# RG-LRU gate products as four 64x64 quadrants of one weight operand, with the halves exchanged on ScalarE

## The chip, the core and the metric

One core of a Trainium2 chip runs the whole program. Its engines are TensorE (PE in the profile; its weight loads are PEld), VectorE (DVE), ScalarE (ACT), GpSimd (POOL) and SyncE (SP). The metric is the device time of one execution in microseconds (us), as the median of three runs.

## The reference

A trunk of two layers over 512 latent and 256 context tokens (768 together), model width 1024. Each layer runs three bidirectional token mixers (HGRN2, mLSTM, RG-LRU), merges them, and then a SwiGLU network. The RG-LRU is 512 channels wide; its gates are block-diagonal products with 8 blocks of 64 channels, for 2 directions (z in the einsum, `d` in the kernel) and 2 gates (g in the einsum, `z` in the kernel: 0 is r, 1 is i):

```
xc = depthwise_conv(lru_x, conv_w, conv_b)
gates = einsum('btnd,zgnde->zgbtne', xc.reshape(b, t, 8, 64), lru_gate_w)   # 2 x 2 gates
gates = gates + lru_gate_b
log_a = -8 * softplus(-lam) * sigmoid(r_pre);  a = exp(log_a)
u = sqrt(max(-expm1(2 * log_a), 0)) * (sigmoid(i_pre) * xc)
h_t = a_t * h_{t-1} + u_t          # forward and backward
```

All data are float32.

## The kernel before

The kernel keeps channels on the 128 partitions and tokens along the free dimension; a line of 768 tokens is cut into 512 and 256 (`ALL`), each in one PSUM bank. Large projections (`dense`, product at L390, tiles `acc`; and `proj_tok`, product at L500) split each float32 operand into two reduced-precision parts and issue three products per tile of weights (`wh` with the high part, `wh` with the low part, `wl` with the high part).

A layer's mixers come one after the other in the program text: four HGRN2 heads (parts `hg`), four RG-LRU blocks of 128 channels (`lru(0)` to `lru(3)`, parts `lru0` to `lru3`; each holds two of the 64-channel blocks), then the gate projections and state preparation of the mLSTM (part `mg`) and the mLSTM (part `ml`). They don't run strictly one after the other: a list scheduler orders the instructions of each engine ahead of time by their readiness and priority, so that projections of the next block lie between the small products of the one before.

In `lru(i)`: the projection to `x` (eviction at L792), a convolution on VectorE into `xc` (tile tag `F`), then the gates. The weight tile `wg` (tag `th`, 128 x 4 x 128) is cleared by GpSimd (L801) and filled on its diagonal by two DMAs, one for each 64-channel block: for each of the four pairs (d, z) a 128x128 matrix with two 64x64 blocks on its diagonal. The product at L812 multiplies it by `xc` in float32 without a split, once per (d, z) and piece of tokens, into a bank of tag `pl` (two buffers, `pl_...` in the rows); ScalarE evicts it with a sigmoid and its bias (L813) into `sg[d][z]` (tag `K`). So a block `i` issues 4 products of 512 columns and 4 of 256, 64 products in all over two layers. After the gates come exp (L819), tanh (L820), square root (L828) on ScalarE, multiplications and scans on VectorE. ScalarE loads another function table (ACT_TABLE_LOAD) whenever the next function isn't in the one that it holds.

The gate biases come in with other per-channel vectors: `vec_dma` (L172) puts 64 rows of 128 into a staging tile, one DMA per vector, and a transpose makes columns of it. Layer 0's DMAs are issued by GpSimd at the start, those of layer 1 some 60 us later; the first gate that needs them starts at 315 us (layer 0) and 1771 us (layer 1).

Other names in the rows: L733 and L750 and L767 are HGRN2 products (tag `mx`), L742 its eviction; L839 evicts the projection of the output gate, L843 its tanh; L881 to L927 prepare the mLSTM's states (L889 and L927 transpose on TensorE, L904 is VectorE's work ahead of L927); L977 and L1002 are the mLSTM's products with 64-channel operands; L1054 is the merge and the SwiGLU network; L210 and L212 split weights.

Of the kernel before, what the change touches and what calls it, by code (L numbers as in the profile page):

```python
# [12 lines left out]
AF = mybir.ActivationFunctionType  # L13
# [33 lines left out]
def trunk_kernel(ctx: ExitStack, tc: tile.TileContext, a: dict, out: bass.AP):  # L47
# [13 lines left out]
    def nm(p):  # L61
        n_names[0] += 1
        return f"{part[0]}{p}{n_names[0]}"
# [3 lines left out]
    def S(tag, n=T, dt=F32, p=128):  # L67
        return pool[0].tile([p, n], dt, tag=tag, name=nm(tag), bufs=BUFS[tag])
# [11 lines left out]
    def small(n, tag, p=128, dt=F32, bufs=4):  # L80
        return sm.tile([p, n], dt, tag=tag, name=nm(tag), bufs=bufs)
# [4 lines left out]
    def mx(dt=F32):  # L86
        return pp.tile([128, 512], dt, tag="mx", name=nm("mx"), bufs=2)

    def pl(dt=F32):
        return pp.tile([128, 512], dt, tag="pl", name=nm("pl"), bufs=2)  # L90
# [11 lines left out]
    V, ACT, G, PE = nc.vector, nc.scalar, nc.gpsimd, nc.tensor  # L102
# [4 lines left out]
    def ldg(o, i):  # L107
        nc.gpsimd.dma_start(o, i)
# [39 lines left out]
    vec = [{}, {}]  # L148
    negb, halfb = [None, None], [None, None]
    vtiles = []  # L150
    for l in range(2):
# [11 lines left out]
        for i, sp_ in enumerate(specs):  # L163
            n = sum(s[2] for s in sp_)
            vt_ = const.tile([128, n], F32, name=f"vec{l}{i}")
            vtiles.append((sp_, vt_, n))
            r = 0
# [4 lines left out]
    def vec_dma(i, q=ld):  # L172
        sp_, vt_, n = vtiles[i]
        st = small(128, "vst", bufs=2)
        r = 0
        for name, src, k in sp_:
            q(st[r:r + k], src)
            r += k
        return st

    def vec_load(i, st=None):
        _, vt_, n = vtiles[i]
        st = st or vec_dma(i, ldg)
        ps = pl()
        PE.transpose(ps[:, :n], st[:n], ident[:n, :n])
        V.tensor_copy(vt_, ps[:, :n])

    ps = pl()
# [12 lines left out]
    V.tensor_reduce(sel, ident.rearrange("p (g m) -> p m g", g=4)[:, 0:2, :], axis=AX.X, op=OP.add)  # L201
    aw_load(0)
    vst0 = vec_dma(0)
    aw_load(2)
    tok_load(0, 2)
# [190 lines left out]
    ALL = ((0, 512), (512, 256))  # L396
# [123 lines left out]
    v0_load(1)  # L520
    vbs = [load_vb(0)]
    vsts = {i: vec_dma(i, ldg) for i in (2, 1)}
    norm_scale(0, 0, 0, 4)
    st_transpose(0, 0)
# [42 lines left out]
    def layer(l, hh, hl):  # L567
# [217 lines left out]
        gw = a["lru_gate_w"][l]  # L785

        def lru(i):
# [5 lines left out]
            xc = S("F")  # L793
            cw = lambda j: vec[l]["conv_w"][:, j * 4 + i:j * 4 + i + 1]
            V.tensor_scalar(xc, x, cw(2), vec[l]["conv_b"][:, i:i + 1], op0=OP.mult, op1=OP.add)
            for s0, s1 in ((0, CTX), (CTX, T)):
                for j, dlt in ((0, -2), (1, -1), (3, 1)):
                    o0, o1 = s0 + max(0, -dlt), s1 - max(0, dlt)
                    V.scalar_tensor_tensor(xc[:, o0:o1], x[:, o0 + dlt:o1 + dlt], cw(j), xc[:, o0:o1], op0=OP.mult, op1=OP.add)
            wg = S("th", 512).rearrange("p (z c) -> p z c", z=4)  # L800
            G.memset(wg, 0.0)  # L801
            for b in range(2):
                ldg(wg[64 * b:64 * b + 64, :, 64 * b:64 * b + 64],
                   gw[:, :, 2 * i + b].rearrange("d z n e -> n (d z) e"))
            sg = []
            for d in range(2):
                sg.append((S("K"), S("K")))
                for z in range(2):
                    bi = (d * 2 + z) * 4 + i
                    for off, n in ALL:  # L810
                        ps = pl()
                        PE.matmul(ps[:, :n], wg[:, 2 * d + z], xc[:, off:off + n], start=True, stop=True)  # L812
                        ACT.activation(sg[d][z][:, off:off + n], ps[:, :n], AF.Sigmoid, bias=vec[l]["gate_b"][:, bi:bi + 1])  # L813
            hs = []
            for d in range(2):
                s_r, s_i = sg[d]
# [19 lines left out]
            th = t2  # L836
# [12 lines left out]
        for i in range(4):  # L849
            lru(i)  # L850
# [34 lines left out]
        for Gx, R in ((Gi, Ri), (Gf, Rf)):  # L885
            for g in range(2):
                ps = mx()
# [35 lines left out]
        for nm_, R in (("cC", Ri), ("cW", Rf), ("cE", m_)):  # L923
            ct = S("col", NCH * 64)
            ps = mx()
# [107 lines left out]
        def B(tag, dt=F32):  # L1033
            return S(tag, no, dt)
# [50 lines left out]
        for n_, (br, zs) in enumerate(((0, za), (2, zc), (1, zb))):  # L1085
            part[0] = f"L{l}br{br}_"
            bh, bl = [], []
            for i in range(4):
                z = B("zt")
# [36 lines left out]
        for m in range(NK):  # L1126
            x = B("bh")
            if l == 0:
# [3 lines left out]
                for g in range(2):  # L1132
                    ps = pl()
# [20 lines left out]
        for off, n in (GA, GB):  # L1154
            st = Stat(n, no)
# [84 lines left out]
        for off, n in (GA, GB):  # L1240
            if l == 0:
                st = Stat(n, no)
# [24 lines left out]
            else:  # L1267
# [5 lines left out]
                for c in range(2):  # L1273
                    cb_ = (off - 256) // GR + 16 * c
                    for hf in range(2):
                        o = og[c][hf]
# [40 lines left out]
```

## Time and profile before

| | |
|---|---|
| median of 3 runs | 2607.26 us (2605.45 to 2610.02) |
| the profiled execution | 2610.73 us |
| its span in the trace | 2609.0 us |
| TensorE busy | 2532.6 us, 97% of the span |
| VectorE / ScalarE / GpSimd busy | 1561.8 / 961.0 / 110.8 us |
| first and last gate product, layer 0 | 315.7 and 400.3 us |
| first and last gate product, layer 1 | 1771.0 and 1859.6 us |

The busy share of an engine is an average over stages with different limits; the stage of the gates is read from its own stretch. Each float32 product is two records ("x2") in the trace. Records of matmuls overlap, since they are pipelined: how long a group really occupies TensorE is read from the start of one row to the start of the next, not from the duration in the row. An idle time stands behind a row in brackets with what ended it.

### The profile page before, as it was taken

What the parts mean: (1) busy time and instruction counts of PE and PEld (TensorE: products, weight loads), DVE (VectorE), ACT (ScalarE), POOL (GpSimd) and SP (SyncE); (2) the same over time, 40 slices, a digit from 0 to 9 for tenths busy, and PEclk for the clock granted to TensorE, in tenths of its full rate; (3) what the DMA queues carried; (4) which work ended last, traced back from release to release, by engine and by line L of the source; (5) the groups of instructions that cost most, each with busy time, mean ns of one, the idle gap of its engine ahead of it and who ended that gap; (6) DMA issues with size and microseconds to landing.
All of it is one profiled execution on the core that took longest, in us unless ns stands there. A gap on an engine that the chain in (4) does not pass through costs nothing.

```text
span 2609.0 us, 36171 instructions
## 1 busy us (share of the span) xinstructions
PE 2532.6 (97%) x14491; PEld 2193.7 (84%) x14491; DVE 1561.8 (60%) x2959; ACT 961.0 (37%) x1462; POOL 110.8 (4%) x213
## 2 busy tenths in 40 slices
PE   8999999998999999999999989999999999999998
PEld 5999878777888888888888889987877889888887
DVE  4677797463666467557445465787865356633335
ACT  4435484232222343212212254448733234422223
POOL 1000010110000100000000010001011000000000
PEclk9999999999999999999999999999999999999999
DMA  7333233433455343335335254653455455333323
GB/s 244 58 47 53 49 66 62 81 77 102 141 130 117 115 128 117 102 105 162 113 107 157 83 127 65 60 57 61 65 86 122 111 107 175 109 97 97 97 91 112
DMA packets 247480, 264.42 MB, mean 101 GB/s; under 512 B 12328, under 2 KB 213360, under 8 KB 247312
## 3 DMA queue, kind: packets, MB, share of 16 engines
q1 hardware_dynamic: 236464, 227.75, 37.8%
q0 software_dynamic: 10272, 33.31, 4.1%
q8 instruction: 114, 1.87, 0.3%
q10 hardware_dynamic: 576, 1.05, 0.1%
q14 instruction: 54, 0.44, 0.1%
HBM read 249.91 MB, written 12.16 MB: 100 GB/s over the span
## 4 chain that ended last, share of the span: by engine, by line
PE 54%; issue 4%; DVE 3%; ACT 2%; DMA 1%; POOL 0%; POOLq 0%; ACTq 0%; DVEq 0%
PE L0ffn_acc L1054 20%; PE L1ffn_acc L1054 14%; PE L1br_acc L1054 5%; PE L1hg_acc L390 4%; PE L0out_acc L1054 2%; PE L1mg_acc L500 1%; PE L1hg_pl L711 1%; PE L1ml_acc L390 1%; PE L1lru_acc L390 1%; PE L1out_acc L1054 1%; PE L1v_acc L500 1%; PE L1lru_pl L812 0%; PE L1ml_mx L1014 0%; ACT L0ffn_ny L376 0%; DMA L0ffn_d<-L1lru_o 0%
## 5 line engine op out<-in xcount | busy, mean ns | idle before, releaser
L1054 PE MATMUL L0ffn_acc<-L0out_h,L0ffn_wh 128*128 128x512 f32 (+1 forms) x1408 | 348.0, 339 | 0.5 <-DVE L0out_h L381 0.3
L1054 PEld LDWEIGHTS L0ffn_acc<-L0out_h,L0ffn_wh 128*128 128x128 f32 x1408 | 241.9, 190 | 30.5 <-DVE L0out_h L381 0.7
L1054 PE MATMUL L0ffn_acc<-L0out_h,L0ffn_wl 128*128 128x512 f32 (+1 forms) x704 | 236.5, 337 | 0.0
L1054 PE MATMUL L1ffn_acc<-L1out_h,L1ffn_wh 128*128 128x512 f32 (+1 forms) x736 | 219.8, 381 | 1.8 <-ACT L1out_h L380 0.9
L258 DVE SCALAR_TENSOR_TENSOR ada_ny<-ada_w,csk,ada_ny 128x512 f32<-128x512 f32 x224 | 157.4, 747 | 85.5 <-DMA ada_w<-in_w_ada_dram 84.7
L1054 PE MATMUL L0br_acc<-h,L0br_wh 128*128 128x512 f32 (+1 forms) x768 | 191.5, 340 | 0.0
L210 ACT ACTIVATE L0ffn_wh<-L0ffn_w 128x1024 fp32r<-128x1024 f32 (+1 forms) x76 | 77.1, 1014 | 275.0 <-PE L0ffn_acc L1054 224.7
L212 DVE TENSOR_TENSOR L1ffn_wl<-L1ffn_w,L1ffn_wh 128x1024 fp32r<-128x1024 f32 (+1 forms) x76 | 88.8, 1168 | 141.8 <-ACT L1ffn_wh L210 141.0
L1054 PE MATMUL L0ffn_acc<-L0ffn_hid,L0ffn_wh 128*128 128x256 f32 (+1 forms) x704 | 172.7, 338 | 0.0
L1054 PEld LDWEIGHTS L1ffn_acc<-L1out_h,L1ffn_wh 128*128 128x128 f32 x736 | 136.3, 188 | 28.8 <-DVE L1out_h L381 1.3
L210 ACT ACTIVATE L1ffn_wh<-L1ffn_w 128x1024 fp32r<-128x1024 f32 (+1 forms) x76 | 77.2, 1015 | 197.4 <-PE L1ffn_acc L1054 156.9
L1054 PEld LDWEIGHTS L0br_acc<-h,L0br_wh 128*128 128x128 f32 x768 | 132.1, 190 | 16.8 <-issue 0.3
L1054 PEld LDWEIGHTS L0ffn_acc<-L0out_h,L0ffn_wl 128*128 128x128 f32 x704 | 133.3, 190 | 14.2
L1054 PE MATMUL L1ffn_acc<-L1out_h,L1ffn_wl 128*128 128x512 f32 (+1 forms) x368 | 139.6, 380 | 0.0
L212 DVE TENSOR_TENSOR L0ffn_wl<-L0ffn_w,L0ffn_wh 128x1024 fp32r<-128x1024 f32 (+1 forms) x68 | 80.9, 1190 | 94.1 <-ACT L0ffn_wh L210 93.7
L390 PE MATMUL L0hg_acc<-h,L0hg_wh 128*128 128x384 f32 (+2 forms) x512 | 136.1, 343 | 0.0
L1054 PEld LDWEIGHTS L0ffn_acc<-L0ffn_hid,L0ffn_wh 128*128 128x128 f32 x704 | 121.0, 190 | 14.2
L1054 PE MATMUL L0br_acc<-h,L0br_wl 128*128 128x256 f32 (+1 forms) x384 | 129.7, 338 | 0.0
L1054 PE MATMUL L1br_acc<-L0ffn_h,L1br_wh 128*128 128x512 f32 x384 | 121.2, 394 | 1.5 <-ACT L1br_gt L1073 1.5
L1054 PE MATMUL L1ffn_acc<-L1ffn_hid,L1ffn_wh 128*128 128x512 f32 (+1 forms) x448 | 115.4, 347 | 0.0
L390 PE MATMUL L1hg_acc<-L0ffn_h,L1hg_wh 128*128 128x384 f32 (+1 forms) x384 | 107.9, 360 | 0.0
L1054 PE MATMUL L0ffn_acc<-L0ffn_hid,L0ffn_wl 128*128 128x256 f32 (+1 forms) x304 | 102.4, 337 | 0.0
(710 smaller groups left out, 5910.1 us busy)
## 6 DMA issues: line engine op xcount, KB each, us to landing
ada_w<-in_w_ada_dram SPq DMA_DIRECT2D x80, 512.0 KB, 3.7
L0ffn_w<-in_w_ffn_in_dram SPq DMA_DIRECT2D x44, 512.0 KB, 3.6
L1ffn_w<-in_w_ffn_in_dram SPq DMA_DIRECT2D x44, 512.0 KB, 3.5
L0br_w<-in_w_in_dram SPq DMA_DIRECT2D x24, 512.0 KB, 5.6
L1br_w<-in_w_in_dram SPq DMA_DIRECT2D x24, 512.0 KB, 5.4
L0hg_w<-in_w_in_dram SPq DMA_DIRECT2D x16, 512.0 KB, 8.4
L0out_w<-in_w_out_dram SPq DMA_DIRECT2D x16, 512.0 KB, 3.5
L0ffn_w<-in_w_ffn_out_dram SPq DMA_DIRECT2D x16, 512.0 KB, 3.4
```

The lines of the kernel that those rows point to most:

```text
L210: ACT.activation(wh[:, :n], w[:, :n], AF.Copy)
L212: V.tensor_tensor(wl[:, :n], w[:, :n], wh[:, :n].bitcast(F32), op=OP.subtract)
L258: V.scalar_tensor_tensor(ac[i], wv, csk[:, kk, i:i + 1], ac[i], op0=OP.mult, op1=OP.add)
L390: PE.matmul(ps[:, :n], A[:, k, :], B[k][:, off - ao:off - ao + n], start=(i == 0), stop=(i == 3 * nk - 1))
L500: PE.matmul(ps[:, :n], A[k][:, c * 128:(c + 1) * 128], W[:, k % 4, :], start=k == 0 and i == 0, stop=k == 7 and i == 3 * (k1 - k0) - 1)
L711: PE.matmul(pv[:, j * 128:(j + 1) * 128], ks[:, j * 128:(j + 1) * 128], comp(Q[g], c, j, j + 1), start=True, stop=True)
L1054: PE.matmul(ps[:, :n], A[:, k, sl], Bm[k0 + k][:, off - ao:off - ao + n], start=cnt[key] == 0, stop=cnt[key] == tot - 1)
```

## The change

The gate weights of a block now stay 64 wide: `wg` is 128 x 4 x 64, the first 64 partitions holding one 64-channel block and the other 64 the second. There is nothing to clear, so the memset is gone. Each 128x128 product becomes two 64x64 quadrants, which use 64 partitions of the operand and 64 columns of the array. For the r gate (z = 0) block b writes its own half of the bank (the quadrants on the diagonal); for the i gate (z = 1) block b writes the other half (the quadrants beside the diagonal), so that the four quadrants of one (d, piece of tokens) are four different parts of the array. The r gate is evicted by one sigmoid over 128 partitions as before; the i gate by two sigmoids over 64 partitions each, which put the halves back in place. The bias of the i gate lies with exchanged halves too, so `vec_dma` loads it in pieces: six DMAs in place of one in each layer. The loops are nested the other way: pieces of tokens outside, gates inside.

```diff
         for name, src, k in sp_:
-            q(st[r:r + k], src)
+            if name == "gate_b":
+                for d in range(2):
+                    o = r + 8 * d
+                    q(st[o:o + 4], src[8 * d:8 * d + 4])
+                    for h in range(2):
+                        q(st[o + 4:o + 8, 64 * h:64 * h + 64], src[8 * d + 4:8 * d + 8, 64 - 64 * h:128 - 64 * h])
+            else:
+                q(st[r:r + k], src)
...
-            wg = S("th", 512).rearrange("p (z c) -> p z c", z=4)
-            G.memset(wg, 0.0)
+            wg = S("th", 256).rearrange("p (z c) -> p z c", z=4)
             for b in range(2):
-                ldg(wg[64 * b:64 * b + 64, :, 64 * b:64 * b + 64],
-                   gw[:, :, 2 * i + b].rearrange("d z n e -> n (d z) e"))
+                ldg(wg[64 * b:64 * b + 64], gw[:, :, 2 * i + b].rearrange("d z n e -> n (d z) e"))
             sg = []
             for d in range(2):
                 sg.append((S("K"), S("K")))
-                for z in range(2):
-                    bi = (d * 2 + z) * 4 + i
-                    for off, n in ALL:
-                        ps = pl()
-                        PE.matmul(ps[:, :n], wg[:, 2 * d + z], xc[:, off:off + n], start=True, stop=True)
-                        ACT.activation(sg[d][z][:, off:off + n], ps[:, :n], AF.Sigmoid, bias=vec[l]["gate_b"][:, bi:bi + 1])
+                for off, n in ALL:
+                    pz = [pl() for z in range(2)]
+                    for z in range(2):
+                        for b in range(2):
+                            o = 64 * (b ^ z)
+                            PE.matmul(pz[z][o:o + 64, :n], wg[64 * b:64 * b + 64, 2 * d + z], xc[64 * b:64 * b + 64, off:off + n],
+                                      start=True, stop=True)
+                    gb = lambda z: vec[l]["gate_b"][:, (d * 2 + z) * 4 + i:(d * 2 + z) * 4 + i + 1]
+                    ACT.activation(sg[d][0][:, off:off + n], pz[0][:, :n], AF.Sigmoid, bias=gb(0))
+                    for b in range(2):
+                        o = 64 * (1 - b)
+                        ACT.activation(sg[d][1][64 * b:64 * b + 64, off:off + n], pz[1][o:o + 64, :n], AF.Sigmoid, bias=gb(1)[o:o + 64])
```

In the changed kernel every line below L172 stands 7 lower up to the gates (L390 is L397, L500 is L507); the gate product is L818, the sigmoid of the r gate L821, that of the i gate L824. The new code is ordered by the same scheduler, and each engine's order changes around the gates.

TensorE, layer 0, second block, before (`F` is `xc`, `th` the weights, `acc` the projection of the next blocks): the first six gate products.

```order
L390 MATMUL L0lru_acc_3557<-h_149,L0lru_wh_3552 128x512
L812 MATMUL L0lru_pl_3314<-L0lru_F_3300,L0lru_th_3308 128x512
L812 MATMUL L0lru_pl_3317<-L0lru_F_3300,L0lru_th_3308 128x256
L390 MATMUL L0lru_acc_3557<-h_157,L0lru_wh_3552 128x512
L390 MATMUL L0lru_acc_3557<-h_149,L0lru_wl_3553 128x512
L812 MATMUL L0lru_pl_3320<-L0lru_F_3300,L0lru_th_3308 128x512
L812 MATMUL L0lru_pl_3323<-L0lru_F_3300,L0lru_th_3308 128x256
```

The same place after, where "64x512 x2" is two quadrants in one bank:

```order
L397 MATMUL L0lru_acc_3494<-h_149,L0lru_wl_3464 128x256
L818 MATMUL L0lru_pl_3334<-L0lru_F_3321,L0lru_th_3329 64x512 x2
L818 MATMUL L0lru_pl_3335<-L0lru_F_3321,L0lru_th_3329 64x512 x2
L397 MATMUL L0lru_acc_3494<-h_150,L0lru_wh_3463 128x256
L397 MATMUL L0lru_acc_3494<-h_158,L0lru_wh_3463 128x256
L397 MATMUL L0lru_acc_3494<-h_150,L0lru_wl_3464 128x256
L397 MATMUL L0lru_acc_3494<-h_151,L0lru_wh_3463 128x256
L818 MATMUL L0lru_pl_3343<-L0lru_F_3321,L0lru_th_3329 64x256 x2
L397 MATMUL L0lru_acc_3494<-h_159,L0lru_wh_3463 128x256
```

The four quadrants of 512 columns stand together here, those of 256 in two places with 128-wide products between them.

ScalarE at the same gates, layer 0, second block, before (`K` holds the evicted gates):

```order
L813 ACT_TABLE_LOAD
L813 ACTIVATE L0lru_K_3312<-L0lru_pl_3314,vec_89 128x512
L813 ACTIVATE L0lru_K_3312<-L0lru_pl_3317,vec_89 128x256
L843 ACTIVATE L0lru_sd_3362<-L0lru_sd_3362 128x768
L813 ACTIVATE L0lru_K_3313<-L0lru_pl_3320,vec_89 128x512
L813 ACTIVATE L0lru_K_3313<-L0lru_pl_3323,vec_89 128x256
L819 ACT_TABLE_LOAD
```

and after (L830 is the exponential, L819 before; L799 the eviction of the projection, L217 a split of weights):

```order
L821 ACT_TABLE_LOAD
L821 ACTIVATE L0lru_K_3332<-L0lru_pl_3334,vec_89 128x512
L824 ACTIVATE L0lru_K_3333<-L0lru_pl_3335,vec_89 64x512 x2
L821 ACTIVATE L0lru_K_3332<-L0lru_pl_3343,vec_89 128x256
L830 ACT_TABLE_LOAD
L830 ACTIVATE L0lru_Q_3372<-L0lru_K_3332,nsp_1835 128x768
L824 ACT_TABLE_LOAD
L824 ACTIVATE L0lru_K_3333<-L0lru_pl_3344,vec_89 64x256
L799 ACTIVATE L0lru_q_3461<-L0lru_acc_3494,vec_90 128x256
L217 ACTIVATE L0lru_wh_3794<-L0lru_w_3793 128x1024
L824 ACTIVATE L0lru_K_3333<-L0lru_pl_3344,vec_89 64x256
```

The exponential of the r gate, with its table, now stands between the two pieces of the i gate, and the last half follows two other instructions.

TensorE, layer 1, the last gate products before (`mg_acc` is the projection for the mLSTM):

```order
L812 MATMUL L1lru_pl_16243<-L1lru_F_16209,L1lru_th_16217 128x512
L500 MATMUL L1mg_acc_16505<-L1mg_wh_16492,L0ffn_h_12922 128x272
L500 MATMUL L1mg_acc_16505<-L1mg_wl_16493,L0ffn_h_12914 128x272
L500 MATMUL L1mg_acc_16505<-L1mg_wh_16492,L0ffn_h_12915 128x272
L500 MATMUL L1mg_acc_16505<-L1mg_wh_16492,L0ffn_h_12923 128x272
L812 MATMUL L1lru_pl_16246<-L1lru_F_16209,L1lru_th_16217 128x256
```

and the last two places after:

```order
L818 MATMUL L1lru_pl_16338<-L1lru_F_16296,L1lru_th_16304 64x256 x2
L397 MATMUL L1ml_acc_16883<-L0ffn_h_12972,L1ml_wl_16879 128x512
L397 MATMUL L1ml_acc_16883<-L0ffn_h_12973,L1ml_wh_16878 128x512
L397 MATMUL L1ml_acc_16883<-L0ffn_h_12981,L1ml_wh_16878 128x512
L818 MATMUL L1lru_pl_16339<-L1lru_F_16296,L1lru_th_16304 64x256 x2
```

Before, 139 projection products of `mg_acc` followed the last gate; after, the last gates stand behind all of them, in the first projection of the mLSTM.

## Rows read from the trace of the kernel before

**Rows 1.** The page: busy time and share of an engine; the chain of work that ended last.

```profile
PE 2532.6 (97%) x14491; PEld 2193.7 (84%) x14491; DVE 1561.8 (60%) x2959; ACT 961.0 (37%) x1462; POOL 110.8 (4%) x213
...
PE 54%; issue 4%; DVE 3%; ACT 2%; DMA 1%; POOL 0%; POOLq 0%; ACTq 0%; DVEq 0%
```

**Rows 2.** Busy time by stretch: the gates of layers 0 and 1.

```profile
core 0: us, PE busy (x) PEld busy (x) DVE busy (x) ACT busy (x) POOL busy (x), PEclk, DMA share, GB/s
315.00:405.00 90.00, 88.45 (x503) 72.28 (x502) 76.47 (x109) 81.63 (x107) 7.84 (x18) 1.00 0.35 64
1770.00:1862.00 92.00, 86.21 (x464) 69.32 (x464) 73.10 (x111) 81.97 (x105) 7.77 (x18) 0.96 0.36 55
```

**Rows 3.** Timeline, TensorE, layer 0's first gates: start, duration, engine, line, tiles, shape.

```profile
315.71 1.02 PE L812 MATMUL L0lru_pl<-L0lru_F,L0lru_th 128*128 128x512 f32 x2
316.57 0.49 PE L733 MATMUL L0hg_mx<-ident,L0hg_K 128*128 128x128 f32 x3
```

**Rows 4.** Timeline, TensorE, mLSTM of layer 0: 64-wide products between 128-wide ones.

```profile
471.02 0.49 PE L1002 MATMUL L0ml_pl<-L0ml_q,L0ml_F 64*128 64x128 f32 x4
471.44 0.73 PE L390 MATMUL L0ml_acc<-h,L0ml_wh 128*128 128x512 f32 x2
...
474.17 1.32 PE L977 MATMUL L0ml_mx<-L0mg_v,L0ml_K 128*64 128x129 f32 x20
475.42 0.49 PE L1002 MATMUL L0ml_pl<-L0ml_q,L0ml_F 64*128 64x128 f32 x2
...
476.17 0.40 PE L390 MATMUL L0ml_acc<-h,L0ml_wh 128*128 128x512 f32 x1
476.49 0.49 PE L1002 MATMUL L0ml_pl<-L0ml_q,L0ml_F 64*128 64x128 f32 x2
476.91 0.50 PE L390 MATMUL L0ml_acc<-h,L0ml_wh 128*128 128x512 f32 x1
477.25 0.40 PE L390 MATMUL L0ml_acc<-h,L0ml_wl 128*128 128x512 f32 x1
477.48 0.39 PE L390 MATMUL L0ml_acc<-h,L0ml_wh 128*128 128x512 f32 x1
```

**Rows 5.** Timeline, TensorE, the same stage some us later.

```profile
483.39 0.39 PE L390 MATMUL L0ml_acc<-h,L0ml_wh 128*128 128x512 f32 x1
483.71 0.66 PE L977 MATMUL L0ml_mx<-L0mg_v,L0ml_K 128*64 128x129 f32 x8
484.31 0.50 PE L390 MATMUL L0ml_acc<-h,L0ml_wh 128*128 128x512 f32 x1
484.64 0.40 PE L390 MATMUL L0ml_acc<-h,L0ml_wl 128*128 128x512 f32 x1
```

**Rows 6.** TensorE's waits in layer 1's gates, 1770 to 1862: total, times, longest.

```profile
PE L1lru_pl L812 <- ACT L1lru_K L813: 4.9, 2, 3.0
```

**Rows 7.** Groups of ScalarE's instructions at layer 0's gates, 315 to 405, by shape.

```profile
L813 ACT ACTIVATE L0lru_K<-L0lru_pl,vec 128x512 f32<-128x512 f32 x16 | 11.0, 690 | 1.5 <-PE L0lru_pl L812 0.9
...
L813 ACT ACT_TABLE_LOAD x8 | 10.3, 1283 | 0.1
L813 ACT ACTIVATE L0lru_K<-L0lru_pl,vec 128x256 f32<-128x256 f32 x16 | 7.6, 472 | 0.1
```

**Rows 8.** ScalarE's waits, layer 0, 310 to 430.

```profile
ACT L0ml_wh L210 <- PE L0mg_acc L500: 16.5, 2, 16.1
```

**Rows 9.** TensorE's waits behind layer 0's gates, 405 to 600.

```profile
PE L0ml_mx L644 <- DVE L0ml_o L639: 7.0, 2, 6.7
PE L0ml_mx L1012 <- DVE L0ml_Q L1005: 5.5, 2, 3.7
PE L0mg_mx L927 <- DVE L0mg_K L904: 3.8, 1, 3.8
```

**Rows 10.** GpSimd's memset of the weights (its line in the source view).

```profile
L801 POOL MEMSET L0lru_th<- x4: 524/538/549, 274.9 to 360.3; 128x512 f32 x4
```

## What the trace of before lets one predict

> **What bounds the kernel now.** I read the page first: TensorE is busy 97% of the span and carries over half of the chain that ended last, ScalarE 37% [rows 1]. Then the busy time by stretch, since the mean hides the stage that the change touches. Where the gates are made, TensorE is still the fullest engine (88.45 of 90 us in layer 0, 86.21 of 92 in layer 1), but ScalarE is at 81.63 and 81.97, far above its mean [rows 2]. So whatever TensorE is spared or charged there counts almost in full, and the question about ScalarE is whether its extra work still fits beside. The waits say how close it is: in layer 1 TensorE stands 4.9 us before gate products because ScalarE has not yet emptied a bank of `pl` [rows 6].
>
> The profiled execution is 2610.73 us, its span 2609.0, the median 2607.26. I make the sum against the execution and carry the difference over to the median.
>
> **TensorE: the products themselves.** One gate product of 512 columns occupies TensorE from 315.71 to 316.57, 0.857 us for two passes [rows 3]; one of 256 columns, by half the columns, 0.43. There are 32 of each in two layers: 32 x (0.857 + 0.43) = 41.2 us before.
>
> After, there are 128 quadrants (64 of 512, 64 of 256). A quadrant streams the same columns as a full product, so it takes 0.857 or 0.43 itself; the gain is only in quadrants that run side by side. The trace has pairs that do. The 20 passes of L977, each using half of the columns of the array, start at 474.17 and the next row at 475.42: 1.25 us, ten times 0.125, where a pass of 128 columns needs 0.107, a quarter of the 0.43 of a 512-column pass in rows 3; twenty one after the other would need 2.2 us [rows 4]. And four passes of L1002, on two halves of the rows, take from 471.02 to 471.44, as long as two do (476.49 to 476.91) [rows 4]. Four quadrants at once no row shows; I take them as side by side, since each half is, and keep the other case as a rival.
>
> How many stand together is given by TensorE's order. The 128 quadrants are not 32 groups of four: they form 48 visits, between which 128-wide products lie (23 in layer 0, 25 in layer 1; 42 runs of products before). Seven hold all four quadrants of 512; the rest are pairs, single quadrants, or an i pair of one piece with an r pair of the next. A visit lasts as long as its longest quadrant: 27 visits contain 512 columns, 21 only 256, so 27 x 0.857 + 21 x 0.43 = 32.2 us. That is **9.0 us less** than 41.2.
>
> **TensorE: going to and fro.** A visit changes the shape of the products that the array runs, and rows 4 and 5 price that. From 476.17 to 477.48 there are three intervals with a 128-wide product at either end of one 64-wide visit: L390 to L1002 takes 0.32, L1002 to L390 0.42, L390 to L390 0.34, then 0.23 again. Up to 477.25 that is 1.08 us for two L390 (0.46) and two passes of L1002 (0.22): 0.40 us too many [rows 4]. In the other form, 483.39 to 484.64 is 1.25 us for two L390 (0.46) and four pairs of L977 (0.44): 0.35 too many [rows 5]. Before, gate products were of the same shape as their neighbours and paid nothing. A quadrant is 64 wide both ways; it is nearest to L977, which is 64 wide in the columns that it writes, so I take 0.345 a visit: 48 x 0.345 = **16.6 us more**. By the other row it is 48 x 0.40 = 19.2. The lower end: of the 0.345, 0.09 lies before the visit, 0.10 behind it and 0.15 within (0.60 for 0.44 of passes); if a visit with longer passes hides what lies within, 0.19 is left, 48 x 0.19 = 9.1. Below that nothing in the rows points.
>
> TensorE's net: +16.6 - 9.0 = **+7.5 us**, from +0.1 to +10.2 with these ends.
>
> **ScalarE.** The i gate's eviction is split: 64 sigmoids become 96, 16 more of 512 columns and 16 more of 256 (64 halves in place of 32 whole). One takes 0.690 and 0.472 us [rows 7]; a half has as many elements a partition, so it takes as long; back to back somewhat less, since a pair of 512 and 256 takes 1.05 us from start to start: 16 x (0.59 + 0.36) = 15.2 us, or 18.6 by the durations. ScalarE's order also has 5 more table loads, 61 for 56, at 1.283 us [rows 7]: 6.4 us. Together +21.6 us over two layers, 11 each. Beside it lies TensorE: between first and last gate, in the new order, layer 0 holds 101.1 us of TensorE work against 98.7 of ScalarE (82.5 and 80.4 before), layer 1 106.5 against 87.5 (78.7 and 79.1 before). In layer 0 the extra work moves into the 16.1 us in which ScalarE waits right behind the gates [rows 8], since the last gate now comes later among the `mg` projections. I cost it at nothing. Without that cover each layer would pay up to 11 us.
>
> **The stretch that shifts.** In layer 1 the gates ran from 1771.0 to 1859.6 us, 9.9 us over TensorE's 78.7 of work: the waits on ScalarE (4.9 [rows 6]), and slower rows behind them, where the granted clock of the stretch is 0.96, a mean of its levels of 2.4 and 1.2 GHz, against 1.00 in layer 0 [rows 2]. With 28 us more TensorE work between the same gates and only 8 more of ScalarE, part of this goes: between 0 and -9.9, I take -3, because two banks of `pl` now serve a group of two and the exponential with its table load is queued between the two pieces of the i gate on ScalarE; the bank is held meanwhile, and the next group's quadrants wait for it. What that adds in waits is inside the same term.
>
> Against this: the last gates come later among the projections of `mg` (93 of them left in layer 0, 214 before; none in layer 1, 139 before). So the mLSTM's preparation, whose waits are 3.8 us at L927 and 6.7 at L644 in layer 0 [rows 9], has less projection work to lie behind, and the LRU's tail on VectorE competes with it. Between 0 and +6, I take +3.
>
> **GpSimd and DMA.** Eight memsets at 0.54 us go [rows 10], all long before their weights are used. Five more bias DMAs a layer, at the start and near 67 us, are 250 us and more ahead of the first gate. Both zero: GpSimd is 4% busy [rows 1], and TensorE never waits for a gate's weights.
>
> **Sum.** -9.0 + 16.6 - 3 + 3 = +7.5 us: 2618 for the execution, **2615** by the median.
>
> **The rivals.**
>
> *Not slower: layer 1's waits vanish.* If TensorE's longer work covers ScalarE completely there, and the mLSTM's waits don't grow, the sum is -9.0 + 16.6 - 9.9 = -2.4: **2605**. For it: 106.5 against 87.5 us of work. Against: the waits come from the order around single banks, not from the sums. It decides at 7.5 us regained; with cheaper visits besides (0.25 us) it goes to 2600.
>
> *Pairs yes, fours no.* Then 11 visits in layer 0 and 9 in layer 1, which hold two pairs, take their second one in series: 9 x 0.857 + 11 x 0.43 = 12.4 us more: **2627**. For it: no row shows more than two products at a time. Against: the halves are independent in both directions.
>
> *The quadrants of one bank don't run side by side.* Both quadrants of a gate write one bank from different rows of the array. L977's pairs share a bank but not the rows' halves, L1002's are on different halves and write two banks [rows 4]: this combination isn't in the trace. In series, pairs double: 32.2 becomes 72 (where the second quadrant of r runs beside the first of i) to 82, so +40 to +50: **2660**. Then the change doesn't do what it is built for. The Trainium skill, "TensorEngine Tiling (Array Packing)", section "Gotcha 1: PSUM Pressure", says that different row tiles can't access the same PSUM bank at once; by that the sum would be this one. No row here tests it.
>
> **How the numbers follow.** About 0.2% (5.2 us) is what a measurement of this kernel can tell from no change: within it is 2602.0 to 2612.5. The forecast has 0.48 (2608 to 2622; 0.36 of it above 2612.5, 0.12 within), layer 1's waits vanishing 0.25 (0.15 within, 0.10 faster), no fours 0.17, one bank 0.10. So slower 0.36 + 0.17 + 0.10 = 0.63, same 0.27, faster 0.10. A range from 2602 to 2630 leaves out the bank case and the end of the fast one, 0.2 together. The likeliest case alone is 2608 to 2622, slower or the same.
>
> **What would show it.** Rows of L818: four quadrants of 512 to the next row in about 0.86 + 0.35 us if side by side, 1.7 + 0.35 in pairs, 2.6 or more in series. The intervals of 128-wide rows around a visit: 0.32 to 0.34 rather than 0.23. Between first and last gate: 101 us in layer 0, 104 to 110 in layer 1. TensorE's waits at L818 for L821 or L824: below 5 us in each layer. ScalarE's waits behind the gates of layer 0: a few us rather than 16. L934 (L927 before) in both layers: 4 to 7 us. I am wrong if a visit costs under 0.2 us, if ScalarE's queue stops TensorE for more than 10 us, or if fours don't form.

## The result: 1.5% slower, and where the time came in

The changed kernel takes 2648.4 us (median of 4, 2639.87 to 2654.27) against 2608.6 us (2605.45 to 2612.42) for the kernel before: ratio 1.015, interval 1.0131 to 1.0169, some 40 us slower. The forecast was 2615 and the range ended at 2630. The profiled execution is the shortest of the four, 2639.87 us with a span of 2638.1, and so shows 29 of the 40 us.

The page of the changed kernel, engines as in [rows 1]:

```profile
span 2638.1 us, 36453 instructions
PE 2542.9 (96%) x14619; PEld 2180.7 (83%) x14619; DVE 1563.0 (59%) x2959; ACT 991.8 (38%) x1499; POOL 111.8 (4%) x215
```

TensorE is busy 10 us more in a span that is 29 us longer. So most of the loss is not work. Starts of the same instructions in both traces say where it comes in. Layer 0, gates and mLSTM together, costs 3 us: the first product of layer 1's gates starts at 1773.9 for 1771.0. The last projection of `mg` in layer 1 is 8.0 us late. The last product of the mLSTM is 32 us late (2032.8 for 2000.7), and everything behind it 29.3. So **21 us arise inside the mLSTM of layer 1**, its preparation included, behind the code that was changed.

TensorE's waits there, 1885 to 2040 (who waited, for whom, total us, times, longest), after:

```profile
PE L1ml_mx L651 <- DVE L1ml_o L646: 7.6, 1, 7.6
PE L1ml_mx L1023 <- DVE L1ml_sd L995: 4.9, 1, 4.9
PE L1mg_mx L938 <- DVE L1mg_K L915: 3.7, 1, 3.7
PE L1ml_mx L988 <- DVE L1ml_F L995: 2.0, 1, 2.0
PE L1mg_mx L900 <- DVE L1mg_ks L892: 1.7, 1, 1.7
PE L1ml_mx L988 <- DVE L1ml_sd L995: 0.4, 1, 0.4
```

and in the same work of the kernel before, 1877 to 2010:

```profile
PE L1mg_mx L927 <- DVE L1mg_K L904: 3.8, 1, 3.8
PE L1br_acc L1054 <- ACT L1br_gt L1073: 1.5, 1, 1.5
PE L1ml_mx L977 <- DVE L1ml_sd L984: 0.5, 1, 0.5
PE L1ml_mx L644 <- DVE L1ml_o L639: 0.4, 2, 0.3
PE L1mg_mx L889 <- DVE L1mg_ks L881: 0.2, 1, 0.2
```

20.3 us of waits for 6.4. L938, the wait that I had named (L927 before; the prediction calls it L934), is as it was; the new ones are further on, at L651, L1023 and L988. Busy time by stretch adds the clock (columns as in [rows 2]), after and then the same work before, some 30 us earlier:

```profile
1920.00:1960.00 40.00, 35.66 (x187) 26.64 (x188) 22.70 (x60) 9.45 (x19) 8.02 (x14) 0.87 0.54 81
1960.00:2000.00 40.00, 37.01 (x203) 27.93 (x201) 24.77 (x70) 13.88 (x25) 5.80 (x10) 1.00 0.52 112
2000.00:2040.00 40.00, 29.96 (x125) 22.16 (x126) 18.89 (x60) 10.55 (x26) 2.94 (x5) 0.83 0.30 60
```

```profile
1892.00:1932.00 40.00, 37.37 (x212) 29.50 (x212) 23.93 (x55) 11.28 (x18) 7.41 (x13) 0.96 0.62 100
1932.00:1970.00 38.00, 37.12 (x207) 27.97 (x205) 25.14 (x73) 13.50 (x28) 6.25 (x10) 1.00 0.46 105
1970.00:2008.00 38.00, 36.26 (x171) 26.90 (x170) 20.46 (x65) 11.86 (x27) 2.94 (x5) 1.00 0.47 80
```

In the stretches with its waits TensorE is granted 0.87 and 0.83 on the mean, between its levels of 2.4 and 1.2 GHz, where before it had 0.96 and 1.00. 0.09 and 0.17 of 40 us are up to 10 us more, less what of it fell into waits.

Why the mLSTM is late is read from ScalarE and VectorE. VectorE's last multiplications on the gates (L840) and ScalarE's evictions into the preparation's first tile (L901), after:

```profile
1898.87 0.96 DVE L840 TENSOR_TENSOR L1lru_K<-L1lru_K,L1lru_K 128x768 f32<-128x768 f32 x1 [0.89 <-ACT L1lru_K L839]
1901.54 0.93 DVE L840 TENSOR_TENSOR L1lru_K<-L1lru_K,L1lru_K 128x768 f32<-128x768 f32 x1
```

```profile
1899.31 0.83 ACT L839 ACTIVATE L1lru_K<-L1lru_K 128x768 f32<-128x768 f32 x1
1900.05 0.23 ACT L329 ACTIVATE L1mg_col<-L1mg_col 128x48 f32<-128x48 f32 x1
1900.18 0.47 ACT L901 ACTIVATE L1mg_K<-L1mg_mx 64x384 f32<-64x384 f32 x1
```

and the same eviction before:

```profile
1878.35 0.47 ACT L890 ACTIVATE L1mg_K<-L1mg_mx 64x384 f32<-64x384 f32 x1
```

The preparation's first four tiles have the tag `K`, of which there are four, and the gates of the last block (`lru3`) hold all of them until its multiplications and scans are done. The first L840 ends at 1899.83; the first eviction starts at 1900.18. Before, the last gate product of layer 1 started at 1859.6 and this eviction at 1878.35; after, the last gate product starts at 1891.0. What the eviction reads had long been there. It reads TensorE's transposes of the mLSTM's gates (L900, L889 before), after:

```profile
1885.28 0.60 PE L900 MATMUL L1mg_mx<-ident,L1mg_ks 128*64 128x128 f32 x4
```

and before:

```profile
1877.32 0.60 PE L889 MATMUL L1mg_mx<-ident,L1mg_ks 128*64 128x128 f32 x4
```

From the start of the transposes to the eviction it is 14.9 us after and 1.0 us before. So of the 22 us by which the eviction is late, 8 come with the projections of `mg` and 14 with the wait behind the tail of `lru3`. The whole preparation follows 22 to 29 us late. The projections of the mLSTM that should lie beside it are issued meanwhile: in TensorE's order 133 of them stand ahead of the transposes at L938, where 54 stood ahead of L927.

### The profile page after: what moved, and what is told of

Same layout as the page of the kernel before. It is cut to its first block, busy times and chain, and to the rows that moved or that the text cites. A ratio compares the mean times of both kernels' runs of the same rounds, so it can differ in the third digit from the quotient of the medians.

```text
span 2638.1 us, 36453 instructions
## 1 busy us (share of the span) xinstructions
PE 2542.9 (96%) x14619; PEld 2180.7 (83%) x14619; DVE 1563.0 (59%) x2959; ACT 991.8 (38%) x1499; POOL 111.8 (4%) x215
## 5 line engine op out<-in xcount | busy, mean ns | idle before, releaser
L217 ACT ACTIVATE L0ffn_wh<-L0ffn_w 128x1024 fp32r<-128x1024 f32 (+1 forms) x76 | 77.0, 1014 | 272.9 <-PE L0ffn_acc L1065 216.1
L217 ACT ACTIVATE L1ffn_wh<-L1ffn_w 128x1024 fp32r<-128x1024 f32 (+1 forms) x76 | 77.2, 1016 | 197.4 <-PE L1ffn_acc L1065 156.9
L397 PE MATMUL L0hg_acc<-h,L0hg_wh 128*128 128x384 f32 (+2 forms) x512 | 136.0, 343 | 0.0
L397 PE MATMUL L1hg_acc<-L0ffn_h,L1hg_wh 128*128 128x384 f32 (+1 forms) x384 | 107.8, 359 | 0.0
```

The lines of the kernel that those rows point to most:

```text
L217: ACT.activation(wh[:, :n], w[:, :n], AF.Copy)
L397: PE.matmul(ps[:, :n], A[:, k, :], B[k][:, off - ao:off - ao + n], start=(i == 0), stop=(i == 3 * nk - 1))
```

## Experiments

Theory A: ScalarE's split of the i gate delays the gates, and with them the mLSTM's preparation. Theory B: the loss is TensorE's, in going between 128-wide products and quadrants. Each run has its own comparison with the kernel before; the ratios are to that, with 95% intervals.

### e1: the split alone

```diff
-                for z in range(2):
-                    for off, n in ALL:
-                        ps = pl()
-                        PE.matmul(ps[:, :n], wg[:, 2 * d + z], ...)
-                        ACT.activation(sg[d][z][:, off:off + n], ps[:, :n], AF.Sigmoid, ...)
+                for off, n in ALL:
+                    pz = [pl() for z in range(2)]
+                    for z in range(2):
+                        PE.matmul(pz[z][:, :n], wg[:, 2 * d + z], ...)
+                    ACT.activation(sg[d][0][:, off:off + n], pz[0][:, :n], AF.Sigmoid, bias=gb(0))
+                    for b in range(2):
+                        o = 64 * b
+                        ACT.activation(sg[d][1][o:o + 64, off:off + n], pz[1][o:o + 64, :n], AF.Sigmoid, ...)
```

> The 128x128 products of before stay (and the memset, and one bias DMA); only the loops are nested as after, with two banks per piece of tokens, and the i gate is evicted by two 64-partition sigmoids, each half in its own place. Theory A (the split sigmoids delay the gates; in the new order the last gates of layer 1 stand behind all of mg, and the mLSTM runs out of projections to lie behind): the loss of after appears without any quadrant, 20 to 40 us, 2630 to 2648 us, with the last L1 mLSTM products 20 us or more late. Theory B (the loss comes from TensorE going between 128-wide products and quadrants): nothing, 2604 to 2613 us.

Measured 2634.5 us, 1.0092 (1.0077 to 1.0107): 24 us without a single quadrant. Theory A holds for these 24 of the 40 us. The trace has the picture of after: the last gate product of layer 1 is 27.5 us later than before, the preparation's first eviction 25.8 (1904.2), the end of the mLSTM 27.4, and this although the last projection of `mg` is only 1.0 us late.

### e2: the quadrants without the split

```diff
-                    for b in range(2):
-                        o = 64 * (1 - b)
-                        ACT.activation(sg[d][1][64 * b:64 * b + 64, off:off + n], pz[1][o:o + 64, :n], ...)
+                    ACT.activation(sg[d][1][:, off:off + n], pz[1][:, :n], AF.Sigmoid, bias=gb(1))
```

> The quadrants of after, all four places of the array, but the i gate is evicted by one 128-partition sigmoid, so its halves stay exchanged (left out: putting them back). ScalarE has 64 sigmoids as before. Theory A: the mLSTM of layer 1 is as early as before, and only TensorE's net of about +7 us is left: 2608 to 2622 us. Theory B: as slow as after, 2640 to 2655 us.

Measured 2616.4 us, 1.002 (1.0009 to 1.0031): 5.5 us slower than before, and 32 us faster than after. TensorE's part of the change is worth about what the sum gave for it (+7.5). The split alone and the quadrants alone make 29 of the 40 us. The other 11 appear only with both together, and no run takes them apart.

### e3: quadrants on the diagonal alone

```diff
-                            o = 64 * (b ^ z)
+                            o = 64 * b
```

> Quadrants on the diagonal for both gates, one 128-partition sigmoid for each, biases as before: nothing to exchange. Only two quadrants can run side by side, so the products take as long as before (41 us), and the visits are paid as in after. Theory A: +16 us of visits at 0.345 us, 2615 to 2630 us. Theory B: 2650 us or more, since nothing is gained for the visits. If visits cost nothing: 2604 to 2613 us.

Measured 2624.3 us, 1.0058 (1.0041 to 1.0075): 13.4 us for 47 visits that save nothing. If all of it is put down to the visits, that is an estimate of 0.28 us each, near the 0.345 of the rows. A kernel with 25 visits in place of 48 (e8: quadrants with whole sigmoids, both gates of 256 columns in one bank) gave no time, so the price wasn't tested by their number. The trace shows what the two other places of the array are worth. Four quadrants of 512 (eight records) and the next row, in e3 and then in after:

```profile
374.29 1.93 PE L811 MATMUL L0lru_pl<-L0lru_F,L0lru_th 64*64 64x512 f32 x8
376.15 0.39 PE L390 MATMUL L0lru_acc<-h,L0lru_wh 128*128 128x256 f32 x1
```

```profile
349.65 1.09 PE L818 MATMUL L0lru_pl<-L0lru_F,L0lru_th 64*64 64x512 f32 x8 [0.61 <-PE L0lru_acc L397]
350.67 0.51 PE L397 MATMUL L0lru_acc<-h,L0lru_wh 128*128 128x256 f32 x2
```

1.86 us in two places, 1.02 in four.

### e4 and e15: one layer at a time

```diff
+            if l == 1:                      # e15: l == 0
+                ... (the changed gates)
+            else:
+                ... (the gates of before)
```

> The change in layer 1 alone; layer 0 as before. Theory A: nearly the whole loss, 25 to 40 us, 2633 to 2648 us. Theory B: about half of it, +12 to +20 us, 2620 to 2629 us, since half of the visits are left.

> The change in layer 0 alone, complement of e4. Theory A: layer 0 pays only TensorE's net and little else, since its mLSTM waits were there before: 0 to +8 us, 2610 to 2619 us. If the layers are alike: 2626 to 2632 us.

Layer 1 alone: 2648.1 us, 1.0141 (1.0117 to 1.0165). Layer 0 alone: 2614.6 us, 1.0007 (0.9994 to 1.002), no difference that the measurement can tell. The same edit costs 37 us in one layer and about 3 in the other, which theory B cannot give.

In e4's trace the end of the mLSTM is slower than in after's (columns as in [rows 2]):

```profile
2000.00:2040.00 40.00, 32.37 (x97) 22.93 (x97) 15.02 (x52) 9.34 (x24) 1.53 (x3) 0.59 0.22 33
```

A granted clock of 0.59 for 0.83, in the same stage. The profiled executions of after and of e4 differ by this more than by anything else; I take it as the likely reason why executions of after spread over 14 us, but no trace of one of its slower executions was taken.

### e5, e14, e6: letting the preparation go ahead

If the preparation is late because it stands behind the tail of `lru3`, it must come back when it doesn't. Two things can hold it: its place in the engines' queues, and its tiles. e5 raises its priority, e14 gives it other tiles, e6 does both.

```diff
+        with tc.high_priority(HOIST):            # e5, e6: l1 = lsmall(...) to colt
...
-        Ri, Rf = S("K", p=64), S("K", p=64)
+        Ri, Rf = S("z", p=64), S("q", p=64)      # e6, e14
-        m_, b_ = S("K", p=64), S("K", p=64)
+        m_, b_ = S("Q", p=64), S("Q", p=64)
-        wi = S("Q", p=64)
+        wi = S("K", p=64)
```

> The changed kernel whole, with a higher priority in the scheduler for the mLSTM's preparation (mg, from the log-sigmoid of its gates to the transposed columns). Theory A1 (that work stands behind the tail of lru3 because its first tiles, tag K, are the four that lru3's gates hold): priority alone moves little, 124 projection products of ml before the transposes of the columns in layer 1 in place of 133 (54 before): 2638 to 2652 us. Rival A2 (it is only queued behind that tail): the loss goes, 2612 to 2625 us.

> The change whole with the tiles of e6 alone, without its priority. In the order 134 projection products of ml stand before the transposes in layer 1, as in after (133; 50 in e6). Theory A1 (both the tiles and the place in the queue hold the preparation back): 2638 to 2654 us, as after. Rival (the tiles alone are the cause, and e6's priority did nothing): 2618 to 2630 us.

> As e5, and the preparation takes its first four tiles from tags that are free by then (z, q, Q, Q; the one that used Q takes K). Now 50 projection products of ml stand before the transposes in layer 1. Theory A1: the waits of the mLSTM in layer 1 go back to those of before and 20 to 30 us come back: 2612 to 2626 us, about as e2. If the loss had nothing to do with the preparation being late: 2640 us or more.

Priority alone 2644.4 us (1.0122, 1.0105 to 1.0138), tiles alone 2640.1 (1.0106, 1.0086 to 1.0126), both 2625.9 (1.0052, 1.0035 to 1.0069). Set against the changed kernel's median, priority gains 4 us, the tiles 8 and both 22 (6, 11 and 25 if each run is set against its own kernel before); the 4 lie within the spread of the runs. The traces say what the times alone don't. Layer 1's preparation, starts in us:

| | transposes of its gates | first eviction | transposes of the columns |
|---|---|---|---|
| before | 1877.3 | 1878.4 | 1894.6 |
| after | 1885.3 | 1900.2 | 1922.3 |
| e5, priority | 1882.1 | 1906.9 | 1923.2 |
| e14, tiles | 1887.3 | 1902.2 | 1924.3 |
| e6, both | 1880.9 | 1882.6 | 1905.3 |

With either hold left, the preparation is as late as in after; with both lifted, the eviction follows its input at once. So each of the two holds it back when the other is lifted, and the 8 us of e14 don't come from an earlier preparation; what they come from was not tested. In e6 the last gate product of layer 1 is even later than in after (34.4 us behind that of before, for 31.4), but the waits of the mLSTM, 1885 to 2040, are down to the size of those of before (7.2 us for 6.4):

```profile
PE L1mg_mx L939 <- DVE L1mg_z L916: 3.8, 1, 3.8
PE L1ml_mx L989 <- DVE L1ml_sd L996: 1.3, 1, 1.3
PE L1ml_pl L1014 <- DVE L1ml_Q L1017: 1.2, 2, 0.7
PE L1ml_mx L651 <- DVE L1ml_o L646: 0.6, 1, 0.6
PE L1ml_mx L989 <- DVE L1ml_F L996: 0.3, 1, 0.3
```

and so is the clock of its second half:

```profile
1960.00:2000.00 40.00, 38.59 (x205) 29.00 (x204) 25.31 (x72) 11.52 (x22) 5.65 (x9) 1.00 0.45 99
2000.00:2040.00 40.00, 39.44 (x182) 31.12 (x181) 19.25 (x46) 16.15 (x28) 4.35 (x8) 1.00 0.62 121
```

### e7: the control

The edit of e6 on the kernel before.

> Control for e6: the kernel before with the same priority and tiles, gates as before. Theory A1: there the preparation was not late, so within 5 us of before, 2604 to 2614 us. If it gains 10 us or more, e6 says nothing on the change itself.

Measured 2614.5 us, 1.0008 (0.9998 to 1.0019). That is 3.5 us above the kernel before by the medians, within what the measurement can tell. Before, the first eviction stood 1 us behind its input, so there was nothing to free; what e6 recovers is the change's own loss.

### e9: the nesting of the loops

e1 without its split: whole sigmoids, pieces of tokens outside, both gates inside.

> The kernel before (128x128 products, whole sigmoids) with only the loops nested as after: pieces of tokens outside, the two gates of a piece in two banks inside. In the order 101 mg products stand behind the last gate of layer 1 (139 before, none in after), 72 of ml before the transposes (54 before, 133 in after), and ScalarE has 7 table loads more. If the split of the sigmoids is what delays the gates: 2609 to 2618 us. If the nesting of the loops is: 2625 us or more, as e1.

Measured 2610.6 us, 0.9993 (0.9984 to 1.0002). Seven more table loads in ScalarE's order and gates that end later among the projections cost nothing that the measurement can tell. What e1 has more than e9 is the split of the sigmoids alone, and it costs 24 us.

### e12: the split, with the preparation freed

e1 with the edit of e6.

> e1 (128x128 products, split sigmoids) with the priority and tiles of e6: 50 projection products of ml before the transposes in layer 1, where e1 had 161. If e1's loss lies in the late preparation: from 2634 to 2610 to 2621 us. What is left above before is what the split costs in the gates' own stage; e6 less this is what the quadrants cost, expected 5 to 10 us. If e1's loss is ScalarE's time itself: 2630 us or more.

Measured 2628.4 us, 1.0064 (1.0046 to 1.0082): a miss. Only 6 of e1's 24 us come back. The early waits are gone, but one is left late in the mLSTM, 1885 to 2040:

```profile
PE L1ml_mx L1016 <- DVE L1ml_o L1026: 3.9, 1, 3.9
PE L1mg_mx L931 <- DVE L1mg_z L908: 3.4, 1, 3.4
PE L1br_acc L1058 <- ACT L1br_gt L1077: 1.5, 1, 1.5
```

and the stretches of 5 us behind it show what it brings with it:

```profile
1990.00:1995.00 5.00, 4.73 (x22) 3.15 (x21) 0.35 (x1) 0.28 (x2) 0.00 (x0) 1.00 0.96 119
1995.00:2000.00 5.00, 1.41 (x4) 1.00 (x4) 2.83 (x12) 1.31 (x4) 0.00 (x0) 0.59 0.17 39
2000.00:2005.00 5.00, 5.00 (x15) 3.63 (x14) 0.68 (x3) 0.54 (x2) 0.00 (x0) 0.50 0.01 3
2005.00:2010.00 5.00, 5.00 (x14) 3.52 (x14) 1.52 (x6) 1.51 (x5) 0.00 (x0) 0.50 0.00 0
2010.00:2015.00 5.00, 5.00 (x17) 3.95 (x16) 2.10 (x7) 1.69 (x2) 0.00 (x0) 0.70 0.00 0
2015.00:2020.00 5.00, 4.86 (x26) 3.72 (x25) 4.52 (x13) 0.00 (x0) 0.16 (x1) 1.00 0.64 58
```

After a wait of 3.9 us TensorE is granted half of its speed (0.50, 1.2 GHz) for ten us and 0.70 in the five behind: about 6.5 us more on top of the 3.9. The row charges the wait to the mLSTM's output, made by VectorE. But VectorE itself had been waiting, for a DMA:

```profile
1996.73 0.61 DVE L1000 SCALAR_TENSOR_TENSOR L1ml_Q<-L1ml_Q,L1mg_col,mlmask 128x128 f32<-128x128 f32 x2 [6.24 <-DMA L1ml_Q<-L1mg_d]
```

This DMA brings in rows that the preparation had written to memory by 1920. GpSimd issues it at 1988.9, after 12.2 us in which it waited (by the profile for ScalarE's L1025), and it takes 7.8 us to land, where the median of its kind is 4.0. A load of weights (`L1br_w`, 512 KB) is issued 0.3 us behind it. In after, the wait of 4.9 us at L1023 has such a DMA behind it too:

```profile
2000.29 0.17 DVE L977 COPY L1ml_mdec<-L1ml_K 128x6 f32<-128x6 f32 x1 [5.51 <-DMA L1ml_K<-L1mg_d]
```

In the kernel before, VectorE waited 2.9 us for these copies in all, in after 12.7. So the freed preparation is not the whole cure. In e12 the transposes of the columns start at 1900.8, only 6 us later than before, and still the last product of the mLSTM is 18 us late (2019.1 for 2000.7): 12 of the 18 us arise behind the preparation, about as much as this wait and the slow stretch behind it. No run changed these copies alone, so their part is read from the traces and not tested; in e6 VectorE waits 11.6 us for them, and TensorE has other work meanwhile.

### e10, e11: the exchange taken off ScalarE

The exchange can be made ahead of the product. Two DMAs write the halves of `xc` exchanged into `x`, which is dead by then; the i gate's weights are loaded on the other halves of the partitions; the quadrants beside the diagonal then write each result in its own place.

```diff
+            for b in range(2):
+                ldg(x[64 * b:64 * b + 64], xc[64 - 64 * b:128 - 64 * b])
...
-                            PE.matmul(pz[z][o:o + 64, :n], wg[64 * b:64 * b + 64, 2 * d + z], xc[64 * b:64 * b + 64, off:off + n],
+                            PE.matmul(pz[z][o:o + 64, :n], wg[k:k + 64, 2 * d + z], (xc, x)[z][k:k + 64, off:off + n],
```

> All four places of the array, but the halves are exchanged ahead of the product: two DMAs write the halves of xc exchanged into x (dead after the convolution), the i gate's weights lie on the other halves of the partitions, and the results come out in place. One 128-partition sigmoid a gate, biases as before, 47 visits. If ScalarE's split was the loss: about as e2, 2611 to 2622 us, with nothing computed wrongly. If quadrants of all four places cost something of their own in the stage: 2635 us or more.

> As e10, with a higher priority for the gates (43 visits) and the priority and tiles of e6 for the mLSTM's preparation (60 projection products of ml before the transposes in layer 1). What the quadrants are worth with the rest out of the way: products 9 us shorter, visits 43 x 0.345 = 15 us, so 2609 to 2619 us by the price of a visit; faster than before by over 5 us only if a visit costs under 0.1 us.

e10: 2624.4 us, 1.0043 (1.0029 to 1.0057), 2 us above its expectation; TensorE now waits for the copies and the issue of the gates here and there (6.5 us at the gates of layer 0, of which 1.7 for the DMAs). e11: 2617.7 us, 1.0024 (1.0014 to 1.0034), as expected. Both compute all, and gain 24 and 31 us on the changed kernel, but not on the one before.

### e13: fewer visits

e6 with a higher priority for the gates too, 39 visits for 48.

> The change whole, with a higher priority for the gates (39 visits in place of 48, 54 table loads in place of 61) and the priority and tiles of e6 (94 projection products of ml before the transposes, 50 in e6). Nine visits less are 3 us: 2615 to 2624 us where e6 had 2626; not faster than before.

Measured 2629.6 us, 1.0072 (1.0057 to 1.0087): 4 us slower than e6, and 5.6 above its expectation. TensorE waits 8.1 us (8 times) for ScalarE ahead of the gates of layer 1, where e6 waits 5.7, and 94 projections stand ahead of the transposes for e6's 50. So the new order takes more than the three us of visits that it saves; which of the two differences does it was not tested.

No kernel of this study beats the one before.

## Why the prediction was wrong, point by point

**The products: right.** I took four quadrants as side by side, without a row for it. They are: eight records in 1.02 us, where one quadrant of 512 alone takes 1.00 (325.94 to 326.94). The rival of pairs falls (its four would take what e3 has, 1.86), and so does that of the bank. The section of the Trainium skill named there, "TensorEngine Tiling (Array Packing)", "Gotcha 1: PSUM Pressure", would have the quadrants of one gate in series, since they come from different row tiles and write one bank; here they write different partitions of the bank and run side by side. The measurement decides. That rival's 2660 lay nearest to the result, by luck: its reason isn't there.

**The visits: right in size.** A visit in the changed kernel:

```profile
363.09 0.39 PE L397 MATMUL L0lru_acc<-h,L0lru_wl 128*128 128x512 f32 x1
363.45 0.65 PE L818 MATMUL L0lru_pl<-L0lru_F,L0lru_th 64*64 64x256 f32 x4
364.03 0.73 PE L397 MATMUL L0lru_acc<-h,L0lru_wh 128*128 128x512 f32 x2
364.60 0.39 PE L397 MATMUL L0lru_acc<-h,L0lru_wl 128*128 128x512 f32 x1
```

0.36 + 0.58 + 0.57 us, for 0.23 + 0.43 + 0.46 of products: 0.39 too many, where I had 0.345 from [rows 5] and 0.40 from [rows 4]. Net of the products e2 gives +5.5 us for +7.5.

**ScalarE "at nothing": the step that failed.** I counted its instructions rightly: 37 more, 32 sigmoids and 5 table loads. Its busy time I had too low: +30.8 us on the page (991.8 for 961.0), where the sum had +21.6. A half takes as long as a whole, in layer 0:

```profile
L824 ACT ACTIVATE L0lru_K<-L0lru_pl,vec 64x512 f32<-64x512 f32 x16 | 10.9, 684 | 0.3
L821 ACT ACTIVATE L0lru_K<-L0lru_pl,vec 128x512 f32<-128x512 f32 x8 | 5.5, 686 | 1.4 <-PE L0lru_pl L818 1.3
```

The cover was the mistake. I asked whether the extra 11 us a layer fit beside TensorE's work and into ScalarE's idle time behind the gates of layer 0 [rows 8], as if ScalarE were a budget. It stands in a chain: gate, exp, tanh, square root, scan, and the tile that this frees. In layer 0 the budget view came out right (the 16.1 us of idle time were used up, and e15 shows no loss). In layer 1 the chain goes on into the mLSTM's preparation through the tiles of tag `K` and the place in the queue. e1 puts 24 us on the split alone, and e6 shows that 22 of the changed kernel's 40 come back when the preparation is let go ahead; in e1's own order only 6 of the 24 do (e12).

**The stretch that shifts: mis-sized, +3 (0 to 6) for 21 us.** I saw in the order that the last gates come behind all of `mg`, and asked at which known wait it would show. I named L927 and read the waits of layer 0 [rows 9]. L938 waits 3.7 us as before; the preparation as a whole moved by 22 us and more, and the loss is at the products behind it, with slower rows after the waits. What I didn't ask is which tiles the preparation's first instruction takes and who holds them. The order could have told the size: 133 projections ahead of the transposes for 54 are 79 products of at most 0.23 us, up to 18 us of cover (an estimate) that is spent before the chain begins.

**Layer 1's waits at the gates, -3: wrong in sign.** TensorE waits 8.2 us at L818 in layer 1, 1770 to 1900, where it waited 4.9 for ScalarE and 0.8 for issue [rows 6]. With two banks for a group of two gates and the exponential queued between the pieces, more work beside them didn't cover it:

```profile
PE L1lru_pl L818 <- ACT L1lru_K L821: 5.9, 3, 4.7
PE L1lru_pl L818 <- PE L1lru_acc L397: 0.9, 1, 0.9
```

So the rival that layer 1's waits vanish falls too. From first to last gate it takes 117.1 us, where I had 104 to 110; that is 10.6 over the 106.5 of TensorE's work, for 9.9 before. Layer 0 takes 106.6, where I had 101. The signs that I had set for being wrong didn't show it: a visit costs over 0.2 us, fours form, and ScalarE stops TensorE for 9.3 us at the gates of both layers together, under the 10. They all look at the gates, and the loss lies behind them.

**GpSimd and the bias DMAs, 0:** nothing in the traces contradicts it: e2 carries both and comes out at TensorE's net.

**What stays open.** e6 is 15 us above before, of which e2 explains 5.5. The rest comes with the split, but the parts don't add up: e12 is 18 above before without quadrants, so that e6 less e12, which was to be the quadrants' cost of 5 to 10 us, is -2.5. The traces tell where it arises: in e6 4 us ahead of layer 1's gates, 6 from there to the last projection of `mg`, and 6 in the mLSTM, of which 4 come back behind it; in e12 12 us in the mLSTM, at the wait on the copy and the slow clock behind it. Open are also the 11 us that split and quadrants cost only together, and the 8 us of e14.

## What to carry to other kernels

Extra work on an engine with idle time is free only if no result of it frees something that the next stage starts with: follow the first tile of the next stage back to who holds it, not only the data. Lifting one hold is not enough where the queue holds the same work too (e5, e14). Where an order is made ahead of time, count the independent work that stands ahead of each chain before and after; cover that is spent early is a loss at the other end. And price a lost microsecond on TensorE at more than itself, since the rows behind a wait may run at the lower clock (6.5 us on top of 3.9 in e12).

## What the runs showed of the hardware

Four 64x64 quadrants, two in each of two PSUM banks, take 1.02 us together, as one alone (1.00), so parts of the array on different rows do write one bank at the same time when their partitions differ. A sigmoid over 64 partitions takes as long as over 128 (684 and 686 ns). A visit of 64x64 products between 128-wide ones costs 0.28 us (an estimate from e3, over the whole kernel) to 0.39 us (rows of after). In e12, after a wait of 3.9 us, the granted clock was 0.50 for ten us. A copy of 256 KB from memory took 7.8 us to land with a 512 KB load of weights issued 0.3 us behind it, where the median of the eight such copies was 4.0 us (e12).
